# Low parts of the weights and the residual's scaling moved from GpSimd to VectorE

## The chip, the cores and the metric

The kernel runs on one core of a Trainium2 chip. The core has a matrix engine (TensorE, PE in the profile; its weight loads are PEld), VectorE (DVE), ScalarE (ACT), GpSimd (POOL) and SyncE (SP), which issues the loads. Each engine works through its own list of instructions in order; between engines only semaphores order the work. The metric is the device time of one execution in microseconds, as the median of several runs.

## The reference, cut to what matters

Two blocks, each of two layers, over 256 tokens of 1024 features. Everything is float32.

```python
def first_block(x, ...):
    for l in range(2):
        # latent, sliding-window and retention attention side by side
        mix = concat([ret_o, swa_o, mla_o]) @ w_out[l]
        x = layer_norm(ALPHA * x + mix, ln1_g[l], ln1_b[l])
        ffn = grouped_moe(x, router_w, router_bias, gate_up[l], down[l])
        x = layer_norm(ALPHA * x + ffn, ln2_g[l], ln2_b[l])

def grouped_moe(x, ...):   # 16 experts in 4 groups: one group per token, 2 experts in it
    h = einsum('td,edf->tef', x, w_gate_up)
    a = silu(h[..., :256]) * h[..., 256:] * gates[..., None]
    return einsum('tef,efd->td', a, w_down)

def second_block(h, ...):
    for l in range(2):
        h = h + 0.5 * swiglu(rms(h), w1, w3, w2)     # first FFN, 2816 wide
        h = h + token_mixer(rms(h), ...)             # windowed attention, pooling, gates
        h = h + 0.5 * swiglu(rms(h), w1, w3, w2)     # second FFN
    return rms(h)
```

## The kernel before

All weights, 331.9 MB with the small tables, are read once and used once. `layout()` packs them in the order of use into tiles of up to 2048 columns by 128 partitions (1024 KB). `Weights.fill` (L339) loads the next tile on SP's queue into one of six buffers, `raw`. A tile is cut into pieces of up to 1024 columns, and each piece is split into two numbers whose sum is the weight: the high part `whi`, a rounding copy on ScalarE (L358), and the low part `wlo = raw - whi` (L360). Both lie in a pool of five buffers each. TensorE then makes three products for every block, high by high, high by low and low by high (`mm3`, recorded under the helper's line L425). A `raw` buffer is free when both parts of its pieces are made, and a piece buffer when TensorE has used it.

Which engine makes a low part is set by a table. The program counts pieces from the start of a phase (the attention's projections, the experts, the first FFN of the second block, the mixer, the second FFN), and `POOL_STEPS` names the counts that go to GpSimd. The last piece of every expert's down projection goes there too. That is 99 of 611 low parts.

The stages follow each other: attention with its norms and softmaxes, `route` (L939 to L987: scores, the group, the token's place `rG`, `rpk`, `pm`), the experts, the second norm, then FFN1, mixer and FFN2. Routing gathers the tokens of a group into 128 slots (`xgh`, `xgl`). An expert is six pieces: four for the gate and up weights (product `ogu`), two for the down weights (product `yg`, summed through `ysp` and `ya`). On VectorE an expert has, beside its low parts, `hh` (the low part of the transposed activations, L508) and `a` (L1160, the product of ScalarE's `sl` with the up half and the gate). After experts 5, 7, 9 and 11 a scaling stands: r times the norm's weight, then plus its bias, for each of two token tiles (L1178 to L1182), one instruction of 128x1024 each, on GpSimd. In the second block the passage from stage to stage runs through a residual sum (`hmx` after the mixer, L1441, `h` after an FFN), a mean of squares, a chain of eight instructions of one column for the root (`f20`, `f21`, L492 to L501) and a split transpose (`xT_f`, `xT_mx`), with `fhh` the high part of an FFN's activations.

The order of instructions on each engine is set by a scheduler that sees the whole program, with priorities from the order of writing. `tc.issue_after(W.on_pool.ins)` adds that what it encloses stands behind GpSimd's latest low part on GpSimd's own list.

Of the kernel before, what the change touches and what calls it, by code (L numbers as in the profile page):

```python
# [17 lines left out]
PSUM = bass.MemoryType.PSUM  # L18

P = 128  # L20
# [19 lines left out]
POOL_STEPS = ((0, 1, 2, 3, 4, 5, 19, 21, 27, 29, 31), (0, 2, 4, 5, 6, 7), (0, 1, 2, 3, 4, 5), (0, 1, 2, 3, 4, 5), (0, 1, 2, 3, 4, 5))  # L40
PHASE = {"cq": 0, "gu": 1, "f1w1": 2, "qk2": 3, "f2w1": 4}
# [6 lines left out]
# ---------------------------------------------------------------------------  # L48
# The order in which the weights are consumed: (array, layer, row, column, width).
# None closes the current DMA tile.  # L50
# ---------------------------------------------------------------------------
# [61 lines left out]
def layout():  # L113
    """Packs the recipe into pieces of at most PIECE columns and DMA tiles of at most RAW."""
# [36 lines left out]
def pack_weights(a):  # L151
    """Lays the weight matrices out in the order of use."""
# [53 lines left out]
# per-partition parameter columns  # L206
# [10 lines left out]
# parameters replicated over the partitions  # L217
# [9 lines left out]
# token-major vectors, one row each  # L227
# [25 lines left out]
# ---------------------------------------------------------------------------  # L253
# Constants that depend on shapes alone.
# ---------------------------------------------------------------------------
# [69 lines left out]
class Weights:  # L325
    """The stream of weights: DMA tiles, each piece split exactly into two float32r parts."""

    def __init__(self, nc, raw, pieces, flat):
        self.nc, self.raw, self.pieces, self.flat = nc, raw, pieces, flat
        self.tiles = layout()[0]  # L330
        self.loaded = []
        self.phase, self.step = 0, 0
        self.segs = self._run()

    def fill(self):
        """Loads the next DMA tile."""
        off, w, t = self.tiles.pop(0)
        r = self.raw.tile([P, RAW], F32, name="raw", tag="raw")
        self.nc.sync.dma_start(out=r[:, :w], in_=self.flat[off : off + w * P].rearrange("(p c) -> p c", p=P))  # L339
        self.loaded.append((r, t))  # L340

    def _run(self):
        nc = self.nc
        while self.tiles or self.loaded:
# [4 lines left out]
            for p in t:  # L349
                n = sum(s[4] for s in p)  # L350
                name = p[0][0]
                if PHASE.get(name, self.phase) != self.phase:
                    self.phase, self.step = PHASE[name], 0
                else:
                    self.step += 1
# [3 lines left out]
                engine = nc.gpsimd if (p is t[-1] and name == "dn") or self.step in self.pool_steps() else nc.vector  # L359
                ins = engine.tensor_tensor(  # L360
                    out=lo[:, :n], in0=r[:, c : c + n], in1=hi[:, :n].bitcast(F32), op=ALU.subtract
                )
                if engine is nc.gpsimd:
                    self.on_pool = ins
# [5 lines left out]

    def pool_steps(self):
        return () if self.phase is None else POOL_STEPS[self.phase]

# [7 lines left out]
def build(ctx: ExitStack, tc: tile.TileContext, ap, tap=None, parts=("b1", "b2")):  # L381
# [41 lines left out]
    # -- small pieces of arithmetic -------------------------------------------------  # L423
# [3 lines left out]
    def mm3(out, a, b, start, stop):  # L427
        """out += a^T b for operands split as (high, low)."""
# [4 lines left out]
    def keep_clock(n):  # L433
        """Products of zeros that nobody reads: the tensor engine halves its clock when it idles."""
# [4 lines left out]
    def gemm_wide(name, x, nk, outs, order=None, nseg=1, tail=1):  # L439
        """Tokens on the partitions: outs[t] is a list of (bank columns, segment columns).  # L440
        The first token tile finishes its last `tail` steps before the second starts them."""
# [11 lines left out]
    def gemm_block(name, x, nk, out):  # L453
        """Features on the partitions, all tokens along the columns."""
# [4 lines left out]
    def gemm_halves(name, x, nk, out):  # L459
        """The same with x = [high | low] along the columns: the result is the sum of out's halves."""  # L460
# [5 lines left out]
    def rsqrt_n(x, r, n, factor):  # L466
        """r = factor / sqrt(x) for [P, n] of positive values."""
# [17 lines left out]
    def rsqrt(x, name, factor=1.0):  # L485
        """factor/sqrt of a [P, 1] column of positive values."""
# [17 lines left out]
    def split_evac(hi, lo, src, scale=None):  # L504
        """hi + lo = src * scale, src in PSUM."""
# [13 lines left out]
    def transpose_scaled(xn, hl, gain):  # L519
        """hl = split of (token-major xn)^T * gain, gain per feature."""  # L520
# [11 lines left out]
    def rms_T(h, gain, name, work, hl=None):  # L532
        """Splits (h * gain)^T; the tokens' factors 1/rms follow where they commute with the
        products: as a column for each token tile and as a row on every partition."""
# [21 lines left out]
    def ln_stats(r, t, name):  # L556
        """Mean and 1/sqrt(var + eps) of the tokens of tile t."""
# [9 lines left out]
    def ln_hat(r, name):  # L567
        """(r - mean) / sqrt(var + eps), token-major."""
# [11 lines left out]
    def affine_T(xh, hl, g, b, work):  # L580
        """hl = split of xh^T * g + b."""
# [18 lines left out]
    def softmax_head(work, sc, width, masks, scales, nsink, sink, name):  # L600
        """sc: PSUM scores of two query tiles side by side, widths given. Returns normalised
        probabilities. scales are the negated factors of the scores."""
# [31 lines left out]
    def swap_halves(src, dst):  # L634
        """Swaps the 32 lower with the 32 upper features of every 64."""
# [3 lines left out]
    def rope(src, swapped, dst, cosT, sinT):  # L639
        """dst = src * cos + swapped * sin."""  # L640
# [5 lines left out]
    # -- block 1 -------------------------------------------------------------------  # L646
    def attention1(l, x, hl, work, cb):
        """x token-major, hl its split transpose. Returns what turns a token tile of x into alpha*x + mix,
        and the router's weights."""
# [10 lines left out]
        # latent projections, tokens on partitions  # L660
# [38 lines left out]
        # transposes of the latents  # L699
        ct = work.tile([P, 2, 5, T], F32R, name="ct", tag="ct")  # L700
        cth, ctl = ct[:, 0], ct[:, 1]
        # per head: 64 features without positions, then the rotated halves of its pair of heads,
        # those of the other head zero in the keys
# [14 lines left out]
        # retention's queries and keys, and the values  # L718
# [15 lines left out]
        # expanded latents  # L734
# [35 lines left out]
        def attend(name, score, vals, masks, scales, sinks, nsinks, first):  # L770
            """Six heads of causal attention, two to each 128-feature block of mix from the given one on.
            The scores of a head are computed ahead of the softmax of the one before."""
# [24 lines left out]
        # latent attention  # L797
# [11 lines left out]
        # sliding-window projections  # L809
# [6 lines left out]
        with tc.issue_after(W.on_pool.ins), tc.issue_after(roped.ins):  # L816
            router = router_weights(l, work)
        # retention
# [3 lines left out]
        for t in range(2):  # L822
            # g * (1 + tanh(g/2)) * gn; the half follows with the group norm
# [4 lines left out]
        with tc.issue_after(W.on_pool.ins), tc.issue_after(roped.ins):  # L828
            rope(rqk, swapped, rqk, cos64, sin64)
# [39 lines left out]
        # sliding-window attention  # L869
# [10 lines left out]
        # output projection and residual  # L880
# [14 lines left out]
    def router_weights(l, work):  # L895
        """The router's weights with the gain of the norm before it taken in, each expert's made
        to sum to 0 over the features (so that they see no mean), and its product with the bias."""
# [15 lines left out]
    def route(rT, stats, router, work):  # L913
        """Router on x1 = norm(r), from r transposed, the norm's scales and the weights above. Returns the group
        one-hot, 256 * group + rank in it, the totals, and a function for the gates."""
# [24 lines left out]
        # group score: the largest sum of two of its experts  # L940
# [18 lines left out]
        # rank of the token among the earlier ones of its group, and the group totals  # L959
# [18 lines left out]
        def gates():  # L978
            # the two best experts inside the group and their normalised scores
# [566 lines left out]
```

## Time and profile before

| | |
|---|---|
| times of three runs | 1811.02, 1812.11, 1816.88 us |
| median | 1812.11 us |
| span of the profiled execution | 1808.4 us |
| that execution's own time, if it is the median run | 1812.11 us, 3.7 us more than its span |
| TensorE busy | 1686.0 us (93%) |
| VectorE busy | 1248.8 us (69%) |
| ScalarE busy | 984.5 us (54%) |
| GpSimd busy | 316.4 us (17%) |
| chain that ended last | TensorE 60%, VectorE 7%, ScalarE 2% |

The span is the time from the first to the last instruction that the profiler recorded. A timeline row gives the start in us from the span's start, the length, the engine, the line, the operation with the tile that it writes and those that it reads, and in brackets the idle time of its engine ahead of it with what ended that. A row of waits says who waited for whom, how long in total, how often, and the longest. A busy TensorE is not one at its peak, and lengths on GpSimd are rough; where a row gathers several instructions, its time is that of all of them.

### The profile page before, as it was taken

The numbers are of one execution on the slowest core, as the hardware profiler recorded it, in microseconds if no ns is written. First come the engines' busy times: TensorE is split into PE (matmuls) and PEld (weight loads), VectorE is DVE, ScalarE is ACT, GpSimd is POOL, SyncE is SP. The second block draws the span as 40 slices with busy tenths as digits, with TensorE's granted clock in tenths as the row PEclk, the third lists the DMA queues.
The fourth block names the chain that finished last, engine by engine and source line by source line (L and its number), as shares of the span: only waits on it lengthen the run. The fifth ranks groups of instructions, "written<-read, shape, count | busy, mean of one in ns | idle before, by whom it ended". The sixth has DMA issues, their size and how long they took to land.

```text
span 1808.4 us, 24789 instructions
## 1 busy us (share of the span) xinstructions
PE 1686.0 (93%) x9258; PEld 1420.2 (79%) x9258; DVE 1248.8 (69%) x2161; ACT 984.5 (54%) x1641; POOL 316.4 (17%) x161
## 2 busy tenths in 40 slices
PE   9897988899889897999899989998999999989997
PEld 8776766788667676888798978887888787968886
DVE  6668788775778878666675576666666666666665
ACT  5644766564456674555555455555555456445553
POOL 2204243512223334000300220003000210130000
PEclk9998999999989999999999989998999999989999
DMA  9332778552148775555352535553555433445540
GB/s 371 135 117 94 285 296 298 210 208 97 70 176 311 303 282 196 207 186 186 135 178 97 194 140 187 186 186 130 196 186 186 163 129 123 172 149 201 187 163 24
DMA packets 49422, 331.86 MB, mean 184 GB/s; under 512 B 5648, under 2 KB 5904, under 8 KB 13712
## 3 DMA queue, kind: packets, MB, share of 16 engines
q1 hardware_dynamic: 47952, 325.73, 49.9%
q10 hardware_dynamic: 1344, 4.49, 0.9%
q8 instruction: 75, 1.23, 0.3%
q14 instruction: 51, 0.42, 0.1%
HBM read 326.79 MB, written 1.05 MB: 181 GB/s over the span
## 4 chain that ended last, share of the span: by engine, by line
PE 60%; DVE 7%; ACT 2%; issue 1%; ACTq 0%; DVEq 0%
PE u L425 13%; PE f L425 13%; PE v L425 12%; PE ogt L425 5%; PE ogu L425 4%; PE obr L425 3%; DVE wlo L360 2%; PE oz L425 2%; PE ovp L425 2%; PE oq L425 2%; ACT whi L358 2%; PE sc L425 1%; PE po L425 1%; DVE fhp L1293 1%; PE opl L425 1%
## 5 line engine op out<-in xcount | busy, mean ns | idle before, releaser
L358 ACT CAST whi<-raw 128x1024 fp32r<-128x1024 f32 (+2 forms) x611 | 629.9, 1033 | 561.7 <-PE v L425 114.7
L360 DVE TENSOR_TENSOR wlo<-raw,whi 128x1024 fp32r<-128x1024 f32 (+5 forms) x512 | 655.8, 1292 | 327.9 <-ACT whi L358 324.7
L360 POOL TENSOR_TENSOR wlo<-raw,whi 128x1024 fp32r<-128x1024 f32 (+4 forms) x99 | 229.5, 2327 | 919.1 <-ACT whi L358 890.8
L425 PE MATMUL f<-whi,fhh 128*128 128x512 f32 x704 | 235.4, 396 | 9.3 <-ACT fhh L1298 8.6
L425 PE MATMUL u<-xT_f,whi 128*128 128x512 f32 x528 | 194.4, 407 | 4.0 <-DVE xT_f L511 4.0
L425 PE MATMUL v<-xT_f,whi 128*128 128x512 f32 x528 | 190.0, 399 | 0.0
L425 PEld LDWEIGHTS f<-whi,fhh 128*128 128x128 f32 x704 | 133.0, 190 | 43.3 <-ACT fhh L1298 10.4
L425 PE MATMUL u<-xT_f,wlo 128*128 128x256 f32 x528 | 150.2, 284 | 0.0
L425 PE MATMUL v<-xT_f,wlo 128*128 128x256 f32 x528 | 148.3, 281 | 0.0
L425 PE MATMUL f<-wlo,fhh 128*128 128x512 f32 x352 | 139.2, 396 | 0.0
L425 PE MATMUL ogu<-wlo,xgh 128*128 128x512 f32 x256 | 105.7, 413 | 24.1 <-DVE wlo L360 24.0
L425 PEld LDWEIGHTS u<-xT_f,whi 128*128 128x128 f32 x528 | 101.8, 193 | 29.1 <-DVE xT_f L511 5.1
L425 PEld LDWEIGHTS v<-xT_f,whi 128*128 128x128 f32 x528 | 99.2, 188 | 24.5
L425 PE MATMUL ogu<-whi,xgl 128*128 128x512 f32 x256 | 101.8, 399 | 5.6 <-DVE xgl L598 5.5
L425 PE MATMUL ogu<-whi,xgh 128*128 128x512 f32 x256 | 104.6, 408 | 0.0
L425 PEld LDWEIGHTS u<-xT_f,wlo 128*128 128x128 f32 x528 | 102.1, 193 | 2.3
L425 PEld LDWEIGHTS v<-xT_f,wlo 128*128 128x128 f32 x528 | 99.8, 189 | 0.0
L425 PE MATMUL ogt<-xT_mx,whi 128*128 128x256 f32 x512 | 97.4, 287 | 0.0
L425 PEld LDWEIGHTS ogu<-wlo,xgh 128*128 128x128 f32 x256 | 49.0, 192 | 47.6 <-DVE wlo L360 39.4
L425 PE MATMUL yg<-whi,hh 128*128 128x512 f32 x256 | 84.6, 391 | 1.2 <-ACT hh L507 1.2
L425 PEld LDWEIGHTS ogt<-xT_mx,whi 128*128 128x128 f32 x512 | 80.4, 191 | 3.0 <-issue 1.5
L425 PEld LDWEIGHTS f<-wlo,fhh 128*128 128x128 f32 x352 | 66.8, 190 | 10.7
(555 smaller groups left out, 3275.7 us busy)
## 6 DMA issues: line engine op xcount, KB each, us to landing
raw<-in_wflat_dram SPq DMA_DIRECT2D x276, 1024.0 KB, 4.8
raw<-in_wflat_dram SPq DMA_DIRECT2D x10, 960.0 KB, 5.6
gb<-in_rows_dram SPq DMA_DIRECT2D x8, 512.0 KB, 4.8
raw<-in_wflat_dram SPq DMA_DIRECT2D x4, 992.0 KB, 4.7
raw<-in_wflat_dram SPq DMA_DIRECT2D x4, 512.0 KB, 3.8
raw<-in_wflat_dram SPq DMA_DIRECT2D x2, 1008.0 KB, 7.0
raw<-in_wflat_dram SPq DMA_DIRECT2D x2, 976.0 KB, 7.8
raw<-in_wflat_dram SPq DMA_DIRECT2D x4, 384.0 KB, 6.4
```

The costliest lines, as they stand in the source:

```text
L358: nc.scalar.copy(hi[:, :n], r[:, c : c + n])
L360: ins = engine.tensor_tensor(out=lo[:, :n], in0=r[:, c : c + n], in1=hi[:, :n].bitcast(F32), op=ALU.subtract)
L425: return TE.matmul(out, lhsT=lhsT, rhs=rhs, start=start, stop=stop)
L1293: V.tensor_tensor(out=hp, in0=row, in1=hp, op=ALU.mult)
```

## The change

All low parts are made on VectorE; the table, the counters and the choice are gone. The scaling of the residual is on VectorE too. What was ordered behind the latest low part on GpSimd is now ordered behind the latest low part, on VectorE; the other engines' instructions inside such a block, GpSimd's among them, have no such order any more. The diff also takes comments away, which moves the line numbers (L360 becomes L351, L358 L350, L508 L494, L1160 L1146, L1182 L1168, L1441 L1427, L492 to L501 become L478 to L487).

```diff
-POOL_STEPS = ((0, 1, 2, 3, 4, 5, 19, 21, 27, 29, 31), (0, 2, 4, 5, 6, 7), (0, 1, 2, 3, 4, 5), ...
-PHASE = {"cq": 0, "gu": 1, "f1w1": 2, "qk2": 3, "f2w1": 4}
...
-                engine = nc.gpsimd if (p is t[-1] and name == "dn") or self.step in self.pool_steps() else nc.vector
-                ins = engine.tensor_tensor(
+                self.split = nc.vector.tensor_tensor(
                     out=lo[:, :n], in0=r[:, c : c + n], in1=hi[:, :n].bitcast(F32), op=ALU.subtract
                 )
-                if engine is nc.gpsimd:
-                    self.on_pool = ins
...
-        with tc.issue_after(W.on_pool.ins), tc.issue_after(roped.ins):
+        with tc.issue_after(W.split.ins), tc.issue_after(roped.ins):
             router = router_weights(l, work)
...
-                    with tc.issue_after(W.on_pool.ins):
-                        G.tensor_tensor(out=r[:, t, :], in0=r[:, t, :], in1=gb[:, j, :], op=op)
+                    with tc.issue_after(W.split.ins):
+                        V.tensor_tensor(out=r[:, t, :], in0=r[:, t, :], in1=gb[:, j, :], op=op)
```

Three places of VectorE's list show what moves. The first is in the experts of layer 0, from the expert after the first group's `ysp`. A row is a line, an operation, the tile it writes and those it reads, and the shape; x5 means five such in a row. Before:

```order
L508 TENSOR_TENSOR ysp<-yg_2214,ysp 128x512
L360 TENSOR_TENSOR wlo<-raw,whi 128x1024 x3
L508 TENSOR_TENSOR hh<-ogu,hh 128x256
L1160 SCALAR_TENSOR_TENSOR a<-ogu,gsl,sl 128x256
L360 TENSOR_TENSOR wlo<-raw,whi 128x1024 x5
L508 TENSOR_TENSOR hh<-ogu,hh 128x256
```

and of the change:

```order
L494 TENSOR_TENSOR ysp<-yg_2214,ysp 128x512
L351 TENSOR_TENSOR wlo<-raw,whi 128x1024 x3
L494 TENSOR_TENSOR hh<-ogu,hh 128x256
L351 TENSOR_TENSOR wlo<-raw,whi 128x1024
L1146 SCALAR_TENSOR_TENSOR a<-ogu,gsl,sl 128x256
L1168 TENSOR_TENSOR x_133<-x_133,gb_1462 128x1024
L351 TENSOR_TENSOR wlo<-raw,whi 128x1024 x2
L494 TENSOR_TENSOR hh<-ogu,hh 128x256
L351 TENSOR_TENSOR wlo<-raw,whi 128x1024 x4
```

An expert's five low parts in a row became six, one of them between `hh` and `a`, and the scaling (`x_133`, `gb`) stands behind `a`, ahead of the next expert's first low parts.

The second place is the first norm of layer 0, ahead of the routing. `ve_ln` is the variance, `ln10` and `ln11` are the root's steps for the two token tiles, `x_133` is the residual. Before:

```order
L564 TENSOR_SCALAR ve_ln_1475<-mv_ln_1471 128x1
L492 TENSOR_SCALAR ln10i<-ve_ln_1475 128x1
L493 TENSOR_SCALAR ln10y<-ln10i 128x1
L496 SCALAR_TENSOR_TENSOR ln10a<-ln10y,ve_ln_1475 128x1
L497 SCALAR_TENSOR_TENSOR ln10y_1480<-ln10a,ln10y 128x1
L498 SCALAR_TENSOR_TENSOR ln10a<-ln10y_1480,ve_ln_1475 128x1
L499 SCALAR_TENSOR_TENSOR ln10y<-ln10a 128x1
L500 SCALAR_TENSOR_TENSOR ln10a<-ln10y,ln10y_1480 128x1
L890 SCALAR_TENSOR_TENSOR x_133<-x_133,oo_1320 128x512
L501 TENSOR_SCALAR ln10r<-ln10a 128x1
L890 SCALAR_TENSOR_TENSOR x_133<-x_133,oo_1321 128x512
```

and of the change:

```order
L550 TENSOR_SCALAR ve_ln_1475<-mv_ln_1471 128x1
L478 TENSOR_SCALAR ln10i<-ve_ln_1475 128x1
L351 TENSOR_TENSOR wlo<-raw,whi 128x1024
L479 TENSOR_SCALAR ln10y<-ln10i 128x1
L876 SCALAR_TENSOR_TENSOR x_133<-x_133,oo_1320 128x512
L482 SCALAR_TENSOR_TENSOR ln10a<-ln10y,ve_ln_1475 128x1
L876 SCALAR_TENSOR_TENSOR x_133<-x_133,oo_1321 128x512
L483 SCALAR_TENSOR_TENSOR ln10y_1480<-ln10a,ln10y 128x1
L547 BN_STATS st_ln_1512<-x_133 128x6
L484 SCALAR_TENSOR_TENSOR ln10a<-ln10y_1480,ve_ln_1475 128x1
L547 BN_STATS st_ln_1512<-x_133 128x6
L485 SCALAR_TENSOR_TENSOR ln10y<-ln10a 128x1
```

A low part of the first expert stands in the first tile's chain, behind `ln10i`, with another behind `ln10y` and a third two rows further down; the residual's sums and the second tile's statistics moved up between the steps.

The third place is the passage from the mixer to the second FFN of layer 0. `hmx` is the residual after the mixer, two halves for each token tile, `ms_f` and `f20` are the mean of squares and the root's steps of the first tile. Before:

```order
L553 TENSOR_SCALAR ms_f_10342<-ss_f_10337 128x1
L492 TENSOR_SCALAR f20i<-ms_f_10342 128x1
L493 TENSOR_SCALAR f20y<-f20i 128x1
L496 SCALAR_TENSOR_TENSOR f20a<-f20y,ms_f_10342 128x1
L497 SCALAR_TENSOR_TENSOR f20y_10347<-f20a,f20y 128x1
L498 SCALAR_TENSOR_TENSOR f20a<-f20y_10347,ms_f_10342 128x1
L499 SCALAR_TENSOR_TENSOR f20y<-f20a 128x1
L500 SCALAR_TENSOR_TENSOR f20a<-f20y,f20y_10347 128x1
L501 TENSOR_SCALAR f20r<-f20a 128x1
L542 TENSOR_SCALAR dg<-cperm,f20r 128x128
L1306 TENSOR_SCALAR hr<-f20r 128x1
L1441 TENSOR_TENSOR hmx<-h_8673,oz_10157 128x512
```

and of the change:

```order
L539 TENSOR_SCALAR ms_f_10342<-ss_f_10337 128x1
L478 TENSOR_SCALAR f20i<-ms_f_10342 128x1
L479 TENSOR_SCALAR f20y<-f20i 128x1
L482 SCALAR_TENSOR_TENSOR f20a<-f20y,ms_f_10342 128x1
L483 SCALAR_TENSOR_TENSOR f20y_10347<-f20a,f20y 128x1
L484 SCALAR_TENSOR_TENSOR f20a<-f20y_10347,ms_f_10342 128x1
L351 TENSOR_TENSOR wlo<-raw,whi 128x1024
L1427 TENSOR_TENSOR hmx<-h_8673,oz_10157 128x512
L1427 TENSOR_TENSOR hmx<-h_8673,oz_10158 128x512
L485 SCALAR_TENSOR_TENSOR f20y<-f20a 128x1
L351 TENSOR_TENSOR wlo<-raw,whi 128x1024
```

The second tile's `hmx` moved up, ahead of the last three steps of the root, and behind one low part that is new on this engine; another follows.

## Rows read from the trace of the kernel before

**Rows 1.** The page, part 1: busy us (share of the span) and instructions.

```profile
PE 1686.0 (93%) x9258; PEld 1420.2 (79%) x9258; DVE 1248.8 (69%) x2161; ACT 984.5 (54%) x1641; POOL 316.4 (17%) x161
```

**Rows 2.** By line and shape: xcount | busy us, mean ns of one.

```profile
L360 DVE TENSOR_TENSOR wlo<-raw,whi 128x1024 fp32r<-128x1024 f32 x482 | 623.3, 1304 | 307.7 <-ACT whi L358 304.6 <-PE orq L425 1.5
...
L360 POOL TENSOR_TENSOR wlo<-raw,whi 128x1024 fp32r<-128x1024 f32 x85 | 203.4, 2399 | 864.6 <-ACT whi L358 836.3 <-issue 13.9 <-PE ogu L425 13.4
```

**Rows 3.** Windows: length, busy us of each engine, clock, DMA share, GB/s.

```profile
180.00:336.00 156.00, 142.90 (x607) 110.45 (x607) 122.03 (x113) 106.44 (x131) 54.47 (x23) 0.98 0.78 282
240.00:249.10 9.10, 8.77 (x38) 6.86 (x38) 7.40 (x8) 6.82 (x9) 3.34 (x2) 1.00 0.90 346
249.10:260.20 11.10, 9.02 (x38) 6.78 (x38) 9.58 (x8) 7.26 (x10) 4.82 (x2) 1.00 0.76 284
```

**Rows 4.** The same view, low parts alone, by engine.

```profile
180.00:336.00 156.00, 73.38 (x180) 34.27 (x180) 105.16 (x73) 41.16 (x19) 0.98 0.78 282
```

**Rows 5.** Waits, 180 to 336 us: us in total, times, longest.

```profile
PEld ogu L425 <- DVE wlo L360: 19.7, 18, 2.1
...
DVE a L1160 <- ACT sl L1159: 12.3, 15, 1.9
PE ogu L425 <- DVE wlo L360: 12.0, 17, 1.7
```

**Rows 6.** Timeline of POOL, 240 to 262 us: start, us, operation.

```profile
245.76 2.42 POOL L360 TENSOR_TENSOR wlo<-raw,whi 128x1024 fp32r<-128x1024 f32 x1 [6.72 <-ACT whi L358]
248.14 3.35 POOL L1182 TENSOR_TENSOR x<-x,gb 128x1024 f32<-128x1024 f32 x1
```

**Rows 7.** Timeline of DVE, the same stretch.

```profile
247.37 7.48 DVE L360 TENSOR_TENSOR wlo<-raw,whi 128x1024 fp32r<-128x1024 f32 x4 [0.45 <-ACT whi L358]
255.18 1.22 DVE L360 TENSOR_TENSOR wlo<-raw,whi 128x1024 fp32r<-128x1024 f32 x1 [0.33 <-ACT whi L358]
```

**Rows 8.** Waits of PE, 131 to 182 us (layer 0, routing).

```profile
PE cn L425 <- DVE rGb L957: 3.7, 1, 3.7
PE ogu L425 <- DVE xgl L598: 2.8, 2, 1.5
PE og L425 <- DVE pm L1055: 2.1, 1, 2.1
```

**Rows 9.** Timeline of DVE, 141 to 155 us.

```profile
141.69 0.23 DVE L926 SCALAR_TENSOR_TENSOR lgs<-lg,ln11r,bsum 128x16 f32<-128x16 f32 x1 [1.05 <-PE lg L425]
...
147.52 2.07 DVE L957 TENSOR_TENSOR rGb<-cperm,rmx 128x8 bf16<-128x8 f32 x1
...
149.70 2.29 DVE L985 TENSOR_TENSOR rpk<-rbi,rG 128x16 f32<-128x16 f32 x2
...
152.34 2.53 DVE L1055 TENSOR_SCALAR pm<-cperm,rslot 128x512 fp32r<-128x512 f32 x2
```

**Rows 10.** Timeline of DVE, 1040 to 1052 us (mixer to FFN2).

```profile
1043.33 0.16 DVE L497 SCALAR_TENSOR_TENSOR f20y<-f20a,f20y 128x1 f32<-128x1 f32 x1
1043.52 2.31 DVE L498 SCALAR_TENSOR_TENSOR f20a<-f20y,ms_f 128x1 f32<-128x1 f32 x1
...
1050.91 1.27 DVE L1441 TENSOR_TENSOR hmx<-h,oz 128x512 f32<-128x512 f32 x2
```

**Rows 11.** Timeline of POOL, the same stretch.

```profile
1043.42 6.98 POOL L360 TENSOR_TENSOR wlo<-raw,whi 128x1024 fp32r<-128x1024 f32 x3 [3.10 <-ACT whi L358]
```

**Rows 12.** Waits of PE, 1020 to 1080 us.

```profile
PE trx L527 <- DVE hmx L1441: 6.5, 1, 6.5
```

**Rows 13.** Waits of PE, 870 to 905 us (FFN1 to mixer).

```profile
PE f L425 <- ACT fhh L1298: 2.8, 1, 2.8
PE oq L425 <- DVE xT_mx L511: 2.0, 1, 2.0
```

**Rows 14.** Waits of PE, 40 to 100 us (attention, layer 0).

```profile
PE ouk L425 <- DVE wlo L360: 5.3, 1, 5.3
```

**Rows 15.** Timeline of POOL, 325 to 345 us (last expert).

```profile
328.64 10.97 POOL L360 TENSOR_TENSOR wlo<-raw,whi 128x1024 fp32r<-128x1024 f32 x6 [6.74 <-PE ogu L425]
```

## What the change is predicted to do

> **What bounds the kernel now.** I read the page's busy shares first, then the waits of TensorE by stretch, then the timelines of VectorE and GpSimd around each wait. TensorE is busy for 93% of the span [rows 1], so 1808.4 − 1686.0 = 122.4 us is all that waits can give back. GpSimd is busy for 17% and by itself holds up almost nothing. The reader is to see in the groups that TensorE mostly waits for VectorE, and that VectorE is late where GpSimd works beside it.
>
> The price of a low part is the first thing to see. On GpSimd one of 128x1024 takes 2399 ns, on VectorE 1304 ns on average [rows 2], but 1.22 us where GpSimd is idle [rows 7]. Four of them beside GpSimd work from 247.37 on took 7.48 us, where 4 x 1.22 = 4.9 would do: 2.6 us more, beside 3.35 us of scaling and the end of a 2.42 us low part on GpSimd [rows 6, 7]. Tiny instructions show it more sharply. In the chain of one column a step takes 0.16 us at 1043.33, and the next, 2.31 us, as soon as GpSimd starts at 1043.42 [rows 10, 11].
>
> [...]
>
> **The change, part by part.** Removed from GpSimd are 99 low parts and 8 scalings; added to VectorE are the same. At 1.22 us each (the scaling has the same shape and two SBUF inputs, so I take the same price; its bounds are 1.22 and GpSimd's own 3.35 us) this is at most 107 x 1.22 = 131 us on VectorE, on top of 1248.8 [rows 1]. TensorE's products stay the same, so only stretches where it waits can change. I go through them.
>
> *Experts, two layers.* In the middle of one layer's experts VectorE is busy 122.0 of 156 us, and 105.2 of that are 73 low parts, 1.44 us each; GpSimd does 19 more [rows 3, 4]. After, 92 low parts at 1.22 are 112.2, the other work stays 122.0 − 105.2 = 16.8, four scalings are 4.9: 133.9 us. So VectorE does a quarter more pieces for 12 us more and still has room. An expert without scaling takes 9.10 us, with TensorE busy 8.77; one with scaling 11.10, which is 2.0 more [rows 3]. The first kind loses its 0.33 us of waiting: the low part that GpSimd made from 245.76 now fits before `a`, and the next expert's first low part is no longer stretched. The second kind loses the stretch, but the scaling stands on VectorE ahead of the next expert's first low part. That one would end at 247.37 + 1.22 + 1.22 = 249.8, against some 249.0 at which TensorE wants it (the present expert ends at 249.1, with the wait in it); I leave 0.8 us. So 16 x 0.33 + 4 x (2.0 − 0.8) = 10.1 us per layer. Bounds: if every scaling keeps its 2.0 us, 5.3; if all of TensorE's and its weight loads' waits go, 12.0 to 19.7 [rows 5]. I take 10, for two layers **20 us** (range 10 to 30).
>
> *Routing, two layers.* TensorE waits 3.7 us for `rGb`, 2.1 for `pm`, 2.8 for `xgl` [rows 8]. GpSimd's low parts stretch `rGb` to 2.07 us, the two `rpk` to 2.29 and the two `pm` to 2.53 [rows 9]. Undisturbed I put them at 0.2, 0.3 and 1.27, from steps of as few columns (0.16 and 0.23) and from two `hmx` of 512 columns (1.27) [rows 9, 10]: 1.9 + 2.0 + 1.3 = 5.2 us of stretch. I let 2.0 of the 2.8 for `xgl` go too. Against it three low parts now stand in the norm's chains ahead of the logits, 3 x 1.22 = 3.7 us, of which the 1.05 us that VectorE waited for the logits [rows 9] is cover. 5.2 + 2.0 − 2.6 = 4.6, and I take 4.5 a layer: **9 us** (0 to 15). The stretch by the centring (L1032) stays.
>
> *Mixer to second FFN, two layers.* Here the step at 1043.52 and two like it take 6.8 us beside GpSimd's three low parts, and the second tile's `hmx` stands behind them until 1050.91, so that TensorE waits 6.5 us for it [rows 10 to 12]. After, the chain is short, one low part stands ahead of `hmx`, within the wait for its sums; the 1.27 us of `hmx` itself stay late. I take 5 each: **10 us** (6 to 13).
>
> *The three other passages between FFN and mixer* (two from FFN1 to mixer, one from FFN2 to FFN1) each show waits of 2.8 and 2.0 us or a little more [rows 13], beside GpSimd's low parts. These now stand in VectorE's gaps. Part of a wait is the chain's own length; I take 2.7 each, **8 us** (0 to 15).
>
> *Attention, two layers.* TensorE waits 5.3 us for a low part on VectorE [rows 14], queued behind rotation steps that GpSimd stretches; layer 1 has a like wait at its own place. The rope's own GpSimd step stays, so I take half: **5 us** (0 to 9). At the very start TensorE waits once for a GpSimd low part, which I put at 0.5.
>
> *End of the experts, two layers.* Six low parts ran hidden on GpSimd, 10.97 us [rows 15]. Now two or three stand between the last sums and the second norm, 1.22 us each, partly in gaps: **−3 us** (−6 to 0).
>
> On the queues: SP loads two tiles fewer ahead of the branch on the group sizes, and they follow behind it; the tiles needed first are there, so nothing. GpSimd keeps rope, centring and the norm's weight, and is free earlier for them.
>
> Sum: 20 + 9 + 10 + 8 + 5 + 0.5 − 3 = 49.5. Against the profiled span, 1808.4 − 49.5 = 1758.9. The profiled execution lies around its span by what the median run of 1812.1 has beyond 1808.4, 3.7 us: **1763 us**, 49 less than that median.
>
> **Rivals.**
> *The stream of weights becomes the bound in the experts.* An expert is three tiles of 1024 KB, 3.15 MB. In the expert without scaling the transfers already run at 346 GB/s with a share of 0.90 [rows 3]. At 1.00 that is 384 GB/s, 8.2 us per expert, under TensorE's 8.77. If more than 346 can't be had, experts stay at 9.1 us, only the scalings' 4 x 1.2 = 4.8 a layer is left, and 10.4 us of the sum go: 1773. For it: the share is high. Against: the loads wait for buffers that low parts free.
>
> *The low parts on the chains eat what the stretch returns.* Outside the experts each low part that lands ahead of a waited step costs 1.22 us. If two more such stand in each of the eleven places above, 11 x 2 x 1.22 = 27 us go, which leaves the experts' 20 and little else: 1790. For it: in the routing three do stand there already. Against: most of TensorE's waits have idle time of VectorE in them.
>
> *VectorE becomes the bound of the experts: slower.* It works in order, behind ScalarE's high part, and idles 156 − 122.0 = 34.0 us in the stretch, 12.3 of it ahead of `a`, for ScalarE [rows 3, 5]. With 133.9 us of work it has room for 156 − 133.9 = 22.1 us of idleness; from there on the stretch gets longer. If none of the 34.0 is filled it is 167.9, 12 us per layer more, and with the same blocking elsewhere the other gains are gone: 1812 + 24 = 1836. If the stretch didn't return either, 92 low parts at 1.44 would add another 20 a layer. For it: VectorE's share would be 134 of 146 us. Against: five piece buffers let it run ahead, and its idle time lies where the moved low parts come in.
> [...]
>
> **How the numbers follow.** The forecast has 0.60, with 1748 to 1778 as its own range. The stream as bound has 0.17 (1773), low parts on the chains 0.13 (1790), VectorE as bound 0.10 (1836, and some milder). 0.3% or 5 us is what can be told from no change; between 1807 and 1817 lie the mild forms of the last two, 0.05. So faster 0.87, same 0.05, slower 0.08. The range goes from 1742, which is the sum with most of the upper ends, to 1796, past the second rival.
>
> **What would show it.** Right: no GpSimd low parts; VectorE's mean low part near 1.2 us and its total within 30 us of the present 1249; experts without scaling at 8.8 us, with it at 9.5; TensorE's 6.5 us for `hmx` down to 1 or 2; the column chains at 0.16 to 0.22 a step. Wrong: low parts on VectorE still near 1.4 us; experts at 9.1 with the DMA share near 1.00 (first rival); waits for `rGb`, `xT_mx` and `xT_f` as long as now though nothing is stretched (second); VectorE over 95% busy and TensorE waiting for low parts in every expert (third).

## The result

The changed kernel takes 1743.0 us as the median of four runs (1737.5 to 1746.3), the kernel before 1813.6 us in the same comparison (1811.0 to 1816.9). The ratio is 0.960 with a 95% interval of 0.958 to 0.9625. That is 70 us less, where 49 had been forecast, in the right direction; times the shown median of 1812.1 the ratio gives 1740, just below the range's lower end of 1742. The gain was one and a half times what the sum said.

The profiled execution has a span of 1735.7 us, 72.7 less than before. It is the fastest of the four (1737.5 us), so the stretches below add up to some 2 us more than the medians differ by. On its page, part 1, VectorE has the same busy time as before with 107 instructions more, and GpSimd has a fifth of its own [rows 1]:

```profile
PE 1662.0 (96%) x9258; PEld 1407.9 (81%) x9258; DVE 1251.6 (72%) x2268; ACT 985.8 (57%) x1643; POOL 62.4 (4%) x54
```

The low parts, one group on the same page (all shapes, count, busy us, mean ns), were 655.8 us for 512 on VectorE and are now:

```profile
L351 DVE TENSOR_TENSOR wlo<-raw,whi 128x1024 fp32r<-128x1024 f32 (+2 forms) x611 | 736.6, 1212 | 351.7 <-ACT whi L350 345.8
```

Ninety-nine more cost 81 us, not 99 x 1.22 = 121. Not every low part became shorter: their median was 1225 ns before and is 1225 now, and the mean [rows 2] hides a few long ones. Of 482 low parts of 128x1024, 41 took over 1.3 us before; 4 of 567 do now. The line of the kernel before has the shortest, the median and the longest in ns:

```profile
L360 DVE TENSOR_TENSOR wlo<-raw,whi x512: 284/1225/3589, 19.9 to 1783.7; 128x1024 fp32r<-128x1024 f32 x161, 128x960 fp32r<-128x960 f32 x3, 128x864 fp32r<-128x864 f32 x2, 128x768 fp32r<-128x768 f32 x2
```

VectorE's other instructions became shorter by some 80 us together, which is why its total stayed.

Where the 72.7 us went shows when the starts of the same rows are compared in the two timelines (first sum of the residual, second expert's `a`, last expert's `a`, first product of the next stage):

| stretch | before, us | after, us | difference | forecast |
|---|---|---|---|---|
| attention, layers 0 and 1 | 131.6, 127.9 | 129.1, 121.0 | −9.4 | −5.5 |
| first norm and routing, to the second expert's `a` | 55.9, 57.8 | 47.8, 49.1 | −16.8 | −9 |
| from there to the last expert's `a` | 141.8, 141.7 | 127.4, 127.6 | −28.5 | −20 |
| last expert to the next stage | 17.5, 24.1 | 18.8, 25.9 | +3.2 | +3 |
| mixer's `hmx` to FFN2, twice | 13.4, 13.4 | 7.5, 7.5 | −11.8 | −10 |
| all else of the second block | 1079.5 | 1070.2 | −9.3 | −8 |

The experts, windows of the changed kernel (length, then busy us of each engine, clock, DMA share, GB/s): the middle of layer 0, an expert without scaling and one behind a scaling, beside [rows 3].

```profile
166.00:311.80 145.80, 142.91 (x630) 113.63 (x629) 132.05 (x139) 111.03 (x136) 0.00 (x0) 0.99 0.88 322
222.01:230.42 8.41, 8.41 (x39) 6.84 (x38) 7.95 (x10) 6.79 (x9) 0.00 (x0) 1.00 1.01 386
230.42:239.68 9.26, 8.78 (x40) 7.02 (x39) 8.94 (x10) 6.92 (x9) 0.00 (x0) 1.00 0.91 328
```

The reader is to see two limits close by: VectorE is busy 7.95 of 8.41 us, and the loads run at a share of 1.01 and 386 GB/s, above the 346 that a rival took as the most. The waits of that stretch, beside [rows 5]:

```profile
ACT whi L350 <- PE ogu L411: 21.3, 43, 1.7
...
PEld ogu L411 <- DVE wlo L351: 3.2, 5, 0.7
PE ogu L411 <- DVE wlo L351: 1.9, 4, 0.5
```

TensorE's waits for low parts are nearly gone, 1.9 us for 12.0. ScalarE waits for TensorE to free a piece, as it did before (29.0 us from 180 to 336 us); so in this stretch the pieces are made as fast as TensorE uses them.

The routing's timeline on VectorE, beside [rows 9], shows what was forecast and one thing that wasn't:

```profile
132.18 1.23 DVE L351 TENSOR_TENSOR wlo<-raw,whi 128x1024 fp32r<-128x1024 f32 x1
...
142.53 1.13 DVE L929 TENSOR_TENSOR rpr<-rbi 128x16 f32<-128x16 f32 x1
...
147.10 0.17 DVE L943 TENSOR_TENSOR rGb<-cperm,rmx 128x8 bf16<-128x8 f32 x1
...
148.08 0.87 DVE L1041 TENSOR_SCALAR pm<-cperm,rslot 128x512 fp32r<-128x512 f32 x2
...
150.83 0.16 DVE L1092 CAST mi<-m 128x2 int32<-128x2 f32 x1
```

The low part stands in the norm's chain, `rGb` and `pm` are short, `rpr` takes 1.13 us beside the centring on GpSimd (four instructions, 5.02 us from 141.11 on), where the next step of its shape takes 0.16. The stretch isn't confined to instructions that read two tiles of data: `pm` compares one tile with a column of numbers, and two of them took 2.53 us before and 0.87 now. The number that decides the branch, `mi`, is ready at 150.83, ahead of the gather's splits; in the kernel before it came behind them:

```profile
175.72 0.16 DVE L1106 CAST mi<-m 128x2 int32<-128x2 f32 x1
```

The passage from mixer to FFN2 on VectorE, beside [rows 10]:

```profile
990.76 0.22 DVE L484 SCALAR_TENSOR_TENSOR f20a<-f20y,ms_f 128x1 f32<-128x1 f32 x1
990.90 1.22 DVE L351 TENSOR_TENSOR wlo<-raw,whi 128x1024 fp32r<-128x1024 f32 x1
992.03 1.28 DVE L1427 TENSOR_TENSOR hmx<-h,oz 128x512 f32<-128x512 f32 x2
```

The step that took 2.31 us takes 0.22, and TensorE's wait for `hmx` went from 6.5 us [rows 12] to 0.4.

### The profile page after: what moved, and what is told of

Read it like the earlier page. It is cut to its first block, busy times and chain, and to the rows that moved or that the text cites. A ratio compares the mean times of both kernels' runs of the same rounds, so it can differ in the third digit from the quotient of the medians.

```text
span 1735.7 us, 24721 instructions
## 1 busy us (share of the span) xinstructions
PE 1662.0 (96%) x9258; PEld 1407.9 (81%) x9258; DVE 1251.6 (72%) x2268; ACT 985.8 (57%) x1643; POOL 62.4 (4%) x54
## 3 DMA queue, kind: packets, MB, share of 16 engines
q8 instruction: 75, 1.23, 0.3%
## 4 chain that ended last, share of the span: by engine, by line
PE 66%; DVE 3%; ACT 2%; issue 1%; ACTq 0%; DVEq 0%
PE v L411 14%; PE u L411 14%; PE f L411 14%; PE ogt L411 6%; PE ogu L411 4%; PE obr L411 3%; PE oz L411 2%; PE yg L411 2%; PE ovp L411 2%; PE oq L411 2%; PE sc L411 1%; PE po L411 1%; DVE wlo L351 1%; ACT junk L537 1%; PE opl L411 1%
## 5 line engine op out<-in xcount | busy, mean ns | idle before, releaser
L351 DVE TENSOR_TENSOR wlo<-raw,whi 128x1024 fp32r<-128x1024 f32 (+2 forms) x611 | 736.6, 1212 | 351.7 <-ACT whi L350 345.8
L350 ACT CAST whi<-raw 128x1024 fp32r<-128x1024 f32 (+2 forms) x611 | 629.7, 1034 | 533.5 <-PE v L411 125.8
L411 PE MATMUL ogu<-wlo,xgh 128*128 128x512 f32 x256 | 102.2, 399 | 3.9 <-DVE wlo L351 3.9
L411 PE MATMUL ogt<-xT_mx,wlo 128*128 128x256 f32 x256 | 73.0, 286 | 0.0
L411 PE MATMUL u<-x2hl,whi 128*128 128x512 f32 x176 | 64.7, 406 | 6.2 <-DVE x2hl L584 6.2
```

The source lines that it names most:

```text
L350: nc.scalar.copy(hi[:, :n], r[:, c : c + n])
L351: self.split = nc.vector.tensor_tensor(out=lo[:, :n], in0=r[:, c : c + n], in1=hi[:, :n].bitcast(F32), op=ALU.subtract)
L411: return TE.matmul(out, lhsT=lhsT, rhs=rhs, start=start, stop=stop)
```

## The experiments

**Is it the neighbour on GpSimd?** The first two runs leave VectorE's list as it is in the changed kernel, instruction by instruction, and put work beside it on GpSimd whose result nobody reads.

```diff
...
+                if (p is t[-1] and name == "dn") or self.step in POOL_STEPS[self.phase]:
+                    for d in range(0, n, 256):
+                        m = min(256, n - d)
+                        nc.gpsimd.tensor_tensor(
+                            out=self.scr[:, :m], in0=r[:, c + d : c + d + m], in1=hi[:, d : d + m].bitcast(F32), op=ALU.subtract
+                        )
...
```

> The changed kernel with VectorE's list untouched, and beside it, on GpSimd, a copy of every one of the 99 subtractions that stood there before (in four pieces of 256 columns, into a scratch tile that nobody reads). No low part comes from GpSimd. Theory A (a GpSimd instruction that reads SBUF stops VectorE's instructions with two SBUF inputs): the low parts' mean goes from 1.21 us to 1.4 us or more, ordinary experts from 8.4 to 9.5 us, the whole to about 1800 us (1780 to 1830), although every low part is still made by VectorE. Rival B (the gain is the shorter way of a low part, 1.22 us in place of 2.4): GpSimd's copies hold up nothing, the time stays at 1743 us within 5.

Measured: 1797.7 us (1795.2 to 1802.0), ratio to before 0.991 (0.988 to 0.995). The groups by line of this run, VectorE's low parts and GpSimd's copies:

```profile
L359 DVE TENSOR_TENSOR wlo<-raw,whi 128x1024 fp32r<-128x1024 f32 (+2 forms) x611 | 787.8, 1303 | 339.0 <-ACT whi L358 337.1
...
L365 POOL TENSOR_TENSOR scr<-raw,whi 128x256 bf16<-128x256 f32 (+1 forms) x384 | 441.4, 1149 | 702.0 <-ACT whi L358 553.4 <-issue 119.0 <-ACT row L546 3.0
```

One expert in its timeline, VectorE and then GpSimd:

```profile
234.70 7.50 DVE L359 TENSOR_TENSOR wlo<-raw,whi 128x1024 fp32r<-128x1024 f32 x5
...
233.21 6.77 POOL L365 TENSOR_TENSOR scr<-raw,whi 128x256 bf16<-128x256 f32 x4 [3.83 <-issue]
```

Five low parts take 7.50 us, 1.50 each, and the four GpSimd pieces beside them 1.7 each, where the means of the run are 1.30 and 1.15 us: each side is longer beside the other. Nearly 55 of the 70 us are gone again although every low part that TensorE uses is made on VectorE. Rival B falls as the whole cause. The size isn't that of the kernel before: GpSimd's copies take 441 us, its low parts took 229.5, and whether some of the 15 us that are left come from the shorter way of a low part isn't shown.

```diff
...
+                if (p is t[-1] and name == "dn") or self.step in POOL_STEPS[self.phase]:
+                    nc.gpsimd.tensor_tensor(
+                        out=self.scr[:, :1], in0=r[:, c : c + 1], in1=hi[:, :1].bitcast(F32), op=ALU.subtract
+                    )
+                    for _ in range(8):
+                        nc.gpsimd.memset(self.scr, 0.0)
...
```

> The same places on GpSimd, but there a one-column subtraction (it waits for the piece) and eight fills of 128x256, which read nothing, about 2.4 us together. [...] Theory A in a wide form (any GpSimd work beside VectorE stretches it): as the run with reads, about 1800 us. Rival B: 1743 us.

Measured: 1738.7 us (1736.5 to 1747.0), ratio to before 0.960 (0.957 to 0.964), as the changed kernel. The same two groups:

```profile
L359 DVE TENSOR_TENSOR wlo<-raw,whi 128x1024 fp32r<-128x1024 f32 (+2 forms) x611 | 736.4, 1212 | 350.8 <-ACT whi L358 344.4
...
L367 POOL MEMSET scr<- 128x256 bf16 x792 | 250.0, 316 | 46.5 <-PE gp L426 0.7 <-POOL scr L367 0.5
```

GpSimd is busy with fills for 250 us, more than with its low parts before [rows 2], and VectorE's mean stays at 1212 ns. So it isn't GpSimd's being busy that counts: the mean is 1303 ns beside copies, which read `raw` and `whi`, and 1212 beside fills, which read nothing.

One difference between the two runs remains: the copies also hold the weight's buffers until they are done. The waits leave little to it: over the whole run ScalarE waits 5.0 us for GpSimd to free a piece with the copies, 6.2 us with the fills, and 1.3 us for a loaded tile in both; its waits of which the profile shows no cause are 42.5 and 33.9 us.

**Does the gain split by stage?** Two runs make half of the change each, in the kernel before.

```diff
-                engine = nc.gpsimd if (p is t[-1] and name == "dn") or self.step in self.pool_steps() else nc.vector
+                engine = nc.gpsimd if self.phase != 1 and self.step in self.pool_steps() else nc.vector
...
```

This is the first, with the scaling on VectorE too; in the second the experts' own low parts and the scaling alone stay on GpSimd.

> The kernel before with only the experts' part of the change: the experts' low parts and the scaling on VectorE, the other stages' low parts on GpSimd as before. By the comparison of the two traces the experts gave about 28 us and the routing 16, with 2 lost at the experts' end: 1813.6 - 42 = 1771 us (1765 to 1779). Rival (part of it came from an order that the whole change set): 1785 us or more.

Measured: 1767.3 us (1767.1 to 1767.4), 45.7 less than its comparison of 1813.0.

> The complement: the low parts of attention, FFNs and mixer on VectorE, the experts' low parts and the scaling on GpSimd as before. By the traces attention gave 9.5 us, mixer to FFN2 11.8, the other passages and the mixer some 8: 1813.6 - 29 = 1785 us (1777 to 1792). Rival: if the two parts don't add up to 70 us, order matters; then this one is 1800 us or above.

Measured: 1788.0 us (1784.6 to 1789.0), 25.0 less. Together 70.7, the whole gain: the parts add up within the some 8 us to which the two intervals leave the sum, and no order that only the full change sets is needed for it.

**What do the scaling and VectorE's load cost?**

```diff
+                    tick = tiny.tile([P, 1], F32, name="tick", tag="tick", bufs=1)
+                    now = G.tensor_tensor(out=tick, in0=hh[0][:, :1].bitcast(F32), in1=hh[0][:, 1:2].bitcast(F32), op=ALU.subtract)
-                    with tc.issue_after(W.split.ins):
-                        V.tensor_tensor(out=r[:, t, :], in0=r[:, t, :], in1=gb[:, j, :], op=op)
+                    with tc.issue_after(now.ins):
+                        G.tensor_tensor(out=r[:, t, :], in0=r[:, t, :], in1=gb[:, j, :], op=op)
```

> The changed kernel with only the eight scalings back on GpSimd, each released by its expert's transposed activations (a one-column subtraction of them stands ahead on GpSimd), so 10 us of VectorE's work less. [...] Rival (VectorE's load is what counts in the experts): 8 x 0.85 = 7 us shorter, 1734 us.

Measured: 1748.3 us (1746.0 to 1752.1), ratio to before 0.965 (0.963 to 0.966) against 0.960. I had expected the experts behind a scaling to take about 11 us again, as before [rows 3], in place of 9.3, 14 us in all. The direction is that one, with less than its size: from the second expert's `a` to the last the two layers take 132.0 us each in place of 127.4 and 127.6, 9.0 us of the 14, and the medians differ by 5.3. The experts with a scaling beside them take 10.4 us in place of 8.4, and those behind it 8.3 in place of 9.3. I had compared the former with 9.3. One low part on VectorE and the scaling on GpSimd, each from its timeline:

```profile
230.41 3.10 DVE L351 TENSOR_TENSOR wlo<-raw,whi 128x1024 fp32r<-128x1024 f32 x1
...
230.02 2.41 POOL L1170 TENSOR_TENSOR x<-x,gb 128x1024 f32<-128x1024 f32 x1
```

So a scaling costs 2.0 us on GpSimd and 0.9 on VectorE.

```diff
...
+                with tc.issue_after(W.split.ins):
+                    V.tensor_tensor(out=scr, in0=gb[:, 0, :512], in1=gb[:, 1, :512], op=ALU.add)
```

> The changed kernel with one more subtraction-like instruction of 128x512 (a sum, into a scratch tile that nobody reads, about 0.66 us) on VectorE in each of 15 experts a layer, 30 in all, 20 us of work. It asks how near VectorE is to being the bound: an ordinary expert has it busy 7.95 of 8.41 us. If VectorE is at its limit, each of the 30 costs its length or nearly, 15 to 20 us: 1757 to 1761. If room is left that it can use, an ordinary expert hides 0.46 of the 0.66 us and only the four with scaling pay in full: 22 x 0.2 + 8 x 0.66 = 10 us, 1751. If the pieces ahead hide all: under 3 us.

Measured: 1749.0 us (1744.4 to 1753.7), ratio to before 0.965 (0.963 to 0.967). In the windows an expert without scaling takes 8.73 us, one behind a scaling 9.89, where the changed kernel has 8.41 and 9.26:

```profile
224.27:233.00 8.73, 8.26 (x37) 6.58 (x36) 8.41 (x11) 6.76 (x9) 0.00 (x0) 1.00 0.98 361
233.00:242.89 9.89, 8.94 (x40) 7.18 (x39) 9.55 (x12) 6.86 (x9) 0.00 (x0) 1.00 0.88 326
```

Half of the added 0.66 us is hidden in the ordinary expert, none behind a scaling: VectorE has about 0.3 us of usable room in 8.4. The medians differ by 6.0 us, nearest to the second of the three cases. The rival that it becomes the bound was not far off.

**Can the rest of GpSimd's work go the same way?**

```diff
...
-                E = V if l + 1 == NL and t else G
-                E.tensor_tensor(out=x[:, t, :], in0=xh[:, t, :], in1=gb[:, 0, :], op=ALU.mult)
-                E.tensor_tensor(out=x[:, t, :], in0=x[:, t, :], in1=gb[:, 1, :], op=ALU.add)
+                with tc.issue_after(last.ins):
+                    V.tensor_tensor(out=x[:, t, :], in0=xh[:, t, :], in1=gb[:, 0, :], op=ALU.mult)
+                    V.tensor_tensor(out=x[:, t, :], in0=x[:, t, :], in1=gb[:, 1, :], op=ALU.add)
```

> The changed kernel with what GpSimd still does after the experts (the second norm's weight and bias, L1468 and L1469) on VectorE as well, ordered behind the last split of the transposed activations. Theory A: these four GpSimd instructions stretched the splits to 2.5 us and more; in layer 1 TensorE waited 6.2 us for the first of them. That wait goes to about 3 us, and some 2 us go in layer 0: 1741 - 5 = 1736 us. Rival (these passages are bound by ScalarE and the chain itself): 1741 us.

Measured: 1745.6 us (1743.5 to 1749.8), ratio to before 0.963 (0.961 to 0.964): no gain. The splits did lose their stretch (0.42 us at most, where the longest in the changed kernel's layer 1 takes 2.56); the wait for the first of them in layer 1 fell from 6.2 us to 1.5. Then a new one came. On VectorE:

```profile
650.75 2.35 DVE L1469 TENSOR_TENSOR x<-xh_ln,gb 128x1024 f32<-128x1024 f32 x2
653.02 2.35 DVE L1470 TENSOR_TENSOR x<-x,gb 128x1024 f32<-128x1024 f32 x2
655.29 1.22 DVE L351 TENSOR_TENSOR wlo<-raw,whi 128x1024 fp32r<-128x1024 f32 x1
656.42 0.21 DVE L539 TENSOR_SCALAR ms_f<-ss_f 128x1 f32<-128x1 f32 x1
```

The mean of squares of FFN1 needs `x`, and TensorE waits for its root (PE's waits, 640 to 850 us; the view names no cause, but `rrow` reads the tile made from that root, which ends just before):

```profile
PE rrow L411 <- issue: 7.5, 1, 7.5
```

> The run before this one, and also the low parts of the centred residual (L1018) and the rotation's first product (L628) on VectorE, so that GpSimd keeps only small things. Theory A: the three steps of the routing that took 1.1 to 1.25 us in place of 0.16 become short, 3 us a layer, but four subtractions of 0.65 us and a low part ahead of `pm` come into the same chain: 0 to 2 us less a layer. With the rotation 1 to 2 us in all: 1732 us (1728 to 1738). Rival: VectorE's own queue eats it, 1740 us or above.

(Its diff: the `G.` of L628 and L1018 becomes `V.`.) Measured: 1749.0 us (1746.6 to 1750.1), ratio to before 0.964 (0.963 to 0.965): slower than the changed kernel. The norm and routing got 1.4 us shorter up to `pm`, but five low parts landed inside the chain of small steps behind the gather, and `mi` came at 169.20 in place of 150.83:

```profile
167.99 1.22 DVE L351 TENSOR_TENSOR wlo<-raw,whi 128x1024 fp32r<-128x1024 f32 x1
169.13 0.17 DVE L986 TENSOR_TENSOR rvs<-rvs,rbe 128x8 f32<-128x8 f32 x1
169.20 0.17 DVE L1093 CAST mi<-m 128x2 int32<-128x2 f32 x1
```

The branch reads `mi`: SP waits 2.3 us for it there, and `gsl`, the first step of VectorE behind it, comes at 176.06 in place of 166.76. From `pm` to the first expert's `a` it took 29.0 and 28.8 us in the two layers, where the changed kernel took 21.5 and 23.5. The rival was right.

> The changed kernel with the second norm's weight and bias on VectorE, behind the splits, in layer 0 alone, where nothing reads the result before the end of the next attention; layer 1 as in the changed kernel, since there TensorE waited 7.5 us for a root that needs the result. Theory A: the splits lose their stretch, 3 us: 1741 - 3 = 1738 us. Rival: as the run that moved both layers, no gain, 1741 to 1746 us.

(The diff of two runs above, for layer 0 alone.) Measured: 1741.1 us (1740.3 to 1741.8), ratio to before 0.961 (0.960 to 0.962): the same as the changed kernel within what can be told. The projections of layer 1 take 3.4 us less, as expected, and the attention behind them takes 4.7 more. There TensorE's granted clock is lower (windows of this run, then the same stretch of the changed kernel):

```profile
406.00:411.00 5.00, 4.58 (x17) 3.47 (x17) 0.84 (x2) 0.00 (x0) 0.00 (x0) 0.58 0.63 210
411.00:416.00 5.00, 5.00 (x15) 4.23 (x16) 2.79 (x9) 0.00 (x0) 0.00 (x0) 0.50 0.00 0
```

```profile
409.00:414.00 5.00, 4.79 (x28) 3.99 (x29) 1.88 (x5) 0.00 (x0) 0.00 (x0) 1.00 0.53 198
```

The granted clock is 0.58 and 0.50, where the changed kernel has 1.00 in the same products, though both have TensorE waiting 0.48 and 0.64 us for `sT` shortly before. The run that moved both layers shows the same fall (0.54 from 405.3 to 415.3 us), so its missing gain isn't the root's alone.

**Is part of the routing's gain TensorE's clock?**

```diff
-WARM = (24, 12, 60, 20)
+WARM = (24, 24, 60, 20)
```

> The kernel before with 24 instead of 12 products of zeros ahead of the gather `og`, so that TensorE is busy while it waits 2.13 us for `pm`. In the trace before, the gather's first products are issued every 0.427 us, up to the ninth or later, and then every 0.235. Theory (part of the routing's gain that the sum missed is TensorE's clock after the wait): the products come at 0.235 us from the second or third on, and 1.3 to 1.6 us a layer go, 1813 - 3 = 1810 us. Rival (the pace has another cause, as the operands' arrival): the pace stays and 12 more products only move the gather back, 1813 us or 1 to 2 us above.

Measured: 1818.0 us (1815.6 to 1821.0), ratio to before 1.004 (1.002 to 1.005): 0.4% longer. The gather's first twelve products do come faster, 0.26 us apart on average for 0.39, and the granted clock from 155 to 165 us is 0.97, where it was 0.82 in the kernel before, with 0.50 over the gather's first eight products there (154.63 to 158.05 us); so their pace went with the granted clock. The twelve take 3.28 us in place of 4.84:

```profile
154.97 3.28 PE L425 MATMUL og<-pm,xs 128*128 128x512 f32 x12
```

But nothing is gained by it: TensorE then waits longer for VectorE's splits and for the branch (PE's waits, 131 to 188 us):

```profile
PE gp L425 <- issue: 4.3, 1, 4.3
...
PE ogu L425 <- DVE xgl L598: 3.6, 2, 2.8
```

So in the kernel before the gather's pace alone gains nothing: what follows waits for VectorE's splits and for the branch. Layer 1 has a like wait of 4.7 us for `gp`; why these grew, from 0.9 us in layer 0, was not settled. In the changed kernel the same twelve products are faster as well, at a granted clock of 0.88 (the kernel before, then the change):

```profile
154.63 4.84 PE L425 MATMUL og<-pm,xs 128*128 128x512 f32 x12 [2.13 <-DVE pm L1055]
```

```profile
149.83 3.42 PE L411 MATMUL og<-pm,xs 128*128 128x512 f32 x12
```

What these 1.4 us are worth there, where the splits are no longer stretched, this run doesn't show.

No version beat the changed kernel beyond what the runs can tell.

## Why the prediction was right or wrong

The cause was right: the stretch belongs to the GpSimd work that reads (1797.7 us with copies back, 1738.7 with fills), and the gains lie where the waits had been read. That all of it would go was the author's assumption, and no run shows that: low parts of 128x1024 over 1.3 us went from 41 of 482 to 4 of 567, and `rpr` still takes 1.13 us beside the centring. The scaling's 0.8 us behind VectorE was measured as 0.85 to 0.9; mixer to FFN2 (−11.8 for −10) and the experts' end (+3.2 for +3) came out near their terms. That all else of the second block came near too (−9.3 for −8) is partly luck: the three FFNs with the passages behind them, which the term was for, gave 0.1, 3.7 and 2.9 us, 6.6 in all, and the mixers, which had no term, most of the rest. Three terms were too small.

- *Experts, 20 forecast, 28.5 measured.* The failed step is "the first kind loses its 0.33 us of waiting": TensorE's busy 8.77 us of 9.10 [rows 3] was taken as what an expert needs. It needs 8.41 to 8.5, so an expert without scaling became 0.69 us shorter and not 0.33; the four behind a scaling became 1.15 us shorter beyond that, for the 1.2 forecast. The busy time is no measure of need: it counts a product's whole length of 0.39 to 0.50 us, though in a row the products start 0.23 us apart. TensorE's timeline before, where a low part is late, with the weight load of the late product, and at the same place after:

```profile
239.43 0.39 PE L425 MATMUL ogu<-whi,xgh 128*128 128x512 f32 x1
240.18 0.50 PE L425 MATMUL ogu<-wlo,xgh 128*128 128x512 f32 x1 [0.36 <-DVE wlo L360]
240.51 0.39 PE L425 MATMUL ogu<-whi,xgl 128*128 128x512 f32 x1
...
240.18 0.19 PEld L425 LDWEIGHTS ogu<-wlo,xgh 128*128 128x128 f32 x1 [0.79 <-DVE wlo L360]
```

```profile
223.64 0.40 PE L411 MATMUL ogu<-whi,xgh 128*128 128x512 f32 x1
223.88 0.40 PE L411 MATMUL ogu<-wlo,xgh 128*128 128x512 f32 x1
224.11 0.39 PE L411 MATMUL ogu<-whi,xgl 128*128 128x512 f32 x1
```

From start to start it was 0.75 and 0.33 us, now 0.24 and 0.23: 0.61 us lost in this expert, where the matmul's row of the wait says 0.36 and the weight load's 0.79. Over the stretch TensorE's waits for low parts fell by 10.1 us (12.0 to 1.9) and the weight loads' by 16.5 (19.7 to 3.2) [rows 5]; 14.2 us a layer were gained, between the two and within the bounds that I had set aside for 10.

- *Routing, 9 forecast, 16.8 measured.* The three low parts cost +1.5 us by the logits, where 2.6 were put, and from the logits to the gather's start 3.8 us came back (3.2 of them ahead of `pm`), less than 5.2, since the centring's stretch moved on to `rpr`. The miss lies behind the gather's start: from there to the second expert's `a` layer 0 went from 32.9 to 27.1 us, and I had counted 2.0. All waits for `xgl` went (2.8 [rows 8]), and the chain of the gates no longer stands behind the splits, with `mi` at 150.83 for 175.72. I saw that move in the order and gave it no value. TensorE's clock may have a part: the gather's first twelve products start within 3.0 and 4.1 us in the two layers, for 4.5 and 4.8 before. That their pace alone gains nothing is shown for the kernel before only, by the run with more products of zeros. How the gain divides between stretch, order and clock was not taken apart, so its cause stays open in part.

- *Attention, 5.5 forecast, 9.4 measured.* "I take half" was the step: the rotation on GpSimd stays, but the 5.3 us wait for a low part [rows 14] is gone whole, and the like one in layer 1 (4.0 us). In layer 0 the projections ahead take 3.0 us longer, which the sum did not have.

The rival of the stream is refuted: 386 GB/s in an ordinary expert. The rival of low parts on the chains was true of a spot (+1.5 us ahead of the logits), and in the run with all on VectorE it took 7.5 and 5.2 us between `pm` and the first expert's `a`. The rival of VectorE as the bound was wrong for the change, but 0.66 us more per expert already shows. That GpSimd's reads lengthen VectorE's low parts and its fills don't is what the pair of runs shows: mean low part 1303 and 1212 ns. For an instruction with one tensor input, as `pm`, the pair is no test. Low parts handed to GpSimd, 2399 ns there on average for a median of 1225 on VectorE, gave VectorE nothing: its busy time is 1248.8 us with that help and 1251.6 without.

## What to carry to other kernels

Before sharing elementwise work between VectorE and GpSimd, look at VectorE's shortest instructions beside GpSimd's: here a step of one column took 2.31 us beside GpSimd's low parts and 0.22 without them, and moving them to a VectorE that looked fuller (69% busy for 17%) made the kernel 70 us shorter. Size a wait by the distance from start to start of TensorE's instructions, not by the busy time; where 0.61 us were lost, the matmul's wait row said 0.36 and the weight load's 0.79. Room on VectorE isn't enough for moving more work there: in two runs here the work moved landed ahead of a branch or a root that TensorE waits for, and nothing was gained (1745.6 and 1749.0 us for 1743.0).

## What the runs showed of the hardware

GpSimd's instructions were longer beside VectorE's too. In the run with fills its one-column subtraction took 1.18 us at 220.60 and at 229.00, each time beside a low part of VectorE of 1.23 us that had begun 0.10 us earlier, where the mean of all 99 is 0.76 us; a fill of 128x256, which reads nothing, took 0.32 us on average. TensorE's granted clock fell to 0.50 in one kernel and stayed at 1.00 in another behind the same waits of 0.48 and 0.64 us, and the changed kernel's own runs at a mean clock of 0.983, 0.979 and 0.976 took 1737.5, 1740.2 and 1746 us: a gain of 3 us can't be told from such differences.
